# Turning the heads' outputs on VectorE and ScalarE instead of on TensorE, in a hybrid decoder block

## The chip, the core and the metric

The kernel runs on one core of one Trainium2 chip. The core has several engines that run at the same time, each through its own list of instructions in order: TensorE (matmuls, called PE in the profile, with its weight loads as PEld), VectorE (DVE), ScalarE (ACT), GpSimd (POOL) and SyncE (SP, here used to issue DMA transfers). They wait for each other through semaphores. SBUF is the on-chip memory with 128 partitions; PSUM holds what TensorE writes. The metric is the device time of one execution in microseconds (us), the median over several executions.

## The reference, cut to what matters

The block takes 512 tokens of width 1024, projects them, runs a gated short convolution beside an mLSTM branch with 4 heads, and merges the two. What the change touches is the output of a head: for each head an array of 512 tokens by 512 values, normalised, scaled by a gain per value (`g_head`) and multiplied by two gates, which is then the left factor of a projection.

```python
hb = mlstm_chunkwise(q, k, v, ig, fg)                  # (B, S, H, DV)
hb = rmsnorm(hb, g_head[l].reshape(N_HEADS, DV)).reshape(bsz, s, V_DIM)
yb = jax.nn.sigmoid(o) * hb * jax.nn.silu(zb)
yb = jnp.einsum('bsv,vd->bsd', yb, w_b_out[l])
```

For the last product TensorE contracts over partitions, so the values of a head have to lie on partitions and the tokens along the free dimension. The head itself is computed with tokens on partitions. Each head's 512x512 array therefore has to be transposed.

## The kernel before, in words

All matrix products are made to near fp32 accuracy from three products of rounded parts: each fp32 block is split into a high half (`whi`, ScalarE, L180) and a low half (`wlo`, VectorE, L181), and `mm3` (L233 to L235) multiplies high by high, high by low and low by high. The large products use Strassen's scheme with seven products of half-size blocks; its sums of weight blocks are made partly by accumulating DMAs of GpSimd (L156) and partly by VectorE (`wraw<-wraw`, L185). Weights come through four buffers `wraw`, filled by SyncE (L148).

The order on TensorE, ScalarE, VectorE and GpSimd is the order in which the program is written. It is written around ticks: after each step of matmuls (in the projection stages 12 matmuls of 512 columns, or 24 of 256 columns) `tick` is called. A tick emits, in this order, the first part of the pending sink of the step before (for instance a snapshot `s` or `v` of PSUM on ScalarE and a sum `c` on VectorE), one half of the next block's split, and one piece of each background task in the list `active`. A weight block has two halves and serves two steps, so its split runs one block ahead of the matmuls.

The turn of a head is such a background task. `finish` waits 2 ticks (even heads) or 3 (odd heads) after the head and then goes through `turn`, one piece per tick. Before the change the pieces are: eight TensorE transposes of 128x128 into two PSUM banks `pty` (L810); two scaled copies to SBUF on ScalarE (L805, the scale is `g_head` on partitions) and eight more transposes; two more scaled copies and the store of the turned head to DRAM by GpSimd (`yt_d<-yc`, L813). It is read back much later, in front of the projection.

Two buffers are shared in turn. `y`, the head's output with tokens on partitions (shown as `gty`), lies in the buffer tagged `qk`, and the next q/k block takes that buffer over. `yc`, the turned head, lies in the buffer tagged `vv`; after heads 0 and 2 the same buffer receives `qk_raw`, q and k of the next head read back from DRAM (the task `recut`, which waits 7 ticks, loads on SyncE and cuts into halves with `qk<-qk_raw` on ScalarE and VectorE).

What runs beside the turn: after an even head the Strassen product of the gate weights, whose weight sums are made by VectorE (L185) and whose results go through a sigmoid (`c<-c`, L781) to DRAM (`sg_d`, L782); after head 1 the q/k product of heads 2 and 3; after head 3 the first convolution product with its taps (L399, L401).

Of the kernel before, what the change touches and what calls it, by code (L numbers as in the profile page):

```python
# [9 lines left out]
F32 = mybir.dt.float32  # L10
F32R = mybir.dt.float32r
AF = mybir.ActivationFunctionType
ALU = mybir.AluOpType

P = 128
S = 512
NT = S // P
# [5 lines left out]
DV = 512  # L23
# [6 lines left out]
HC = 4  # L30
# [6 lines left out]
def hybrid_block(ctx, tc, x, p, g_mix, w_in, conv_w, conv_b, w_a_out, b_gates, g_head,  # L37
                 w_b_out, w_o, g_ple, w_ple_gate, w_ple, g_final, out):
    nc = tc.nc
    act, dve, pool, pe = nc.scalar, nc.vector, nc.gpsimd, nc.tensor  # L40
# [7 lines left out]
    ps_x = ctx.enter_context(tc.tile_pool(name="ps_x", bufs=4, space=bass.MemoryType.PSUM))  # L48
    dram = ctx.enter_context(tc.tile_pool(name="dram", bufs=1, space=bass.MemoryType.DRAM))

    def open_pool(name, bufs=1, **kw):
        c = tc.tile_pool(name=name, bufs=bufs, reuse_waits="tile", **kw)
        return c, c.__enter__()
# [16 lines left out]
    H2 = S // 2  # L70
# [182 lines left out]
    ident = const.tile([P, P], F32, name="ident")  # L253
# [270 lines left out]
    gh = prm[:, 40:56]  # L524
# [117 lines left out]
    for g in range(2):  # L642
        src = wg_raw[:, :, g * NH:(g + 1) * NH]
# [57 lines left out]
    B = nc.vector.STREAM_SQUARE_SIZE  # L701
# [96 lines left out]

    def turn(h, y):

        yc = hp.tile([P, 2, 2, HC, H2], F32, name="yc", tag="vv", align_bytes=256)[:, 0]
        pts = {}
        for i in range(3):
            for v in range(2 * i - 2, 2 * i) if i else ():
                act.activation(yc[:, :, v, :], pts[v].rearrange("p (h s) -> p h s", h=2), AF.Copy,  # L805
                               scale=gh[:, 4 * h + v:4 * h + v + 1])
            for v in range(2 * i, 2 * i + 2) if i < 2 else ():
                pts[v] = ps_x.tile([P, S], F32, name="pty", tag="x")
                for t in range(NT):
                    pe.transpose(pts[v][:, t * P:(t + 1) * P], y[:, t, v * P:(v + 1) * P], ident)  # L810
            if i < 2:
                yield
        nc.gpsimd.dma_start(yt_d[h], yc)  # L813

    def qk_tile():
# [181 lines left out]
    def finish(h, y, wait):  # L997
        for _ in range(wait):
            yield
        yield from turn(h, y)  # L1000

    hp_ctx, hp = open_pool("heads")
# [3 lines left out]
    for h in range(NH):  # L1006
        y = head(h, qks[h])
# [395 lines left out]
    q = [slice(CW, CW + CW // 2), slice(CW + CW // 2, D)]  # L1403
# [50 lines left out]
```

## Time and profile before

| | |
|---|---|
| time, median of 3 runs | 845.38 us (844.95 to 847.07) |
| profiled execution | 847.37 us, of which 845.6 us span from the first to the last instruction |
| granted TensorE clock | 0.998 |
| turns of heads 0 to 3, first transpose | 164.7, 257.7, 383.5, 476.5 us |
| stores of the turned heads, issue | 170.55, 266.06, 389.36, 483.29 us |

In rows of the profile a number at the front is the start in us from the first instruction, the next one the duration, then engine, source line, operation, output and inputs, and in square brackets how long the engine had been idle before and what ended that. "Chain of waits" is the chain of work that ended last, followed back from the end. Neighbouring instructions of VectorE and ScalarE can overlap a little, so from start to start they are closer than their durations. In a row of the view by stretches there stand the stretch and its length, then busy time and number of instructions for PE, PEld, DVE, ACT and POOL, the granted clock and the DMA share.

### The profile page before, as it was taken

The page shows a single profiled execution, that of the slowest core. Times are in us where ns is not written, and L with a number is a line of the kernel's source. Part 1 is how long each engine was busy: PE and PEld are TensorE (multiplying, and loading weights), DVE is VectorE, ACT ScalarE, POOL GpSimd, SP SyncE. Part 2 cuts the span into 40 slices and gives each one's busy share as a digit, 9 for nine tenths or more (in the row PEclk, how much of TensorE's full clock was granted, in tenths as well). Part 3 has the DMA queues.
Part 4 walks back from the last instruction along what each step waited for, and adds up shares of the span by engine and source line. Part 5 has one row for each costly group of instructions (what it writes and reads, how often), then busy time and mean ns, then how long its engine had stood idle before and what let it go on. Part 6 is the DMA issues. An engine that isn't in the chain of part 4 may idle for free.

```text
span 845.6 us, 12113 instructions
## 1 busy us (share of the span) xinstructions
PE 834.5 (99%) x4584; PEld 726.7 (86%) x4584; DVE 651.0 (77%) x878; ACT 495.5 (59%) x720; POOL 210.0 (25%) x203
## 2 busy tenths in 40 slices
PE   8999999999999999999999999999999999999996
PEld 7888888887889988888788999999998888888885
DVE  5788767975787677788668779897986677999565
ACT  6467665666865566665776654555453256667543
POOL 5203122203124321220222333433411122131031
PEclk9999999999999999999999999999999999999999
DMA  9748779779978997896898799899989488999402
GB/s 310 269 145 183 159 166 220 194 274 227 252 159 207 244 225 180 199 215 199 258 243 211 156 218 169 194 184 182 181 255 380 101 194 214 284 258 229 187 0 100
DMA packets 103939, 173.89 MB, mean 206 GB/s; under 512 B 5632, under 2 KB 46132, under 8 KB 102600
## 3 DMA queue, kind: packets, MB, share of 16 engines
q0 software_dynamic: 39488, 70.33, 44.6%
q1 hardware_dynamic: 59792, 94.64, 33.7%
q10 hardware_dynamic: 4600, 8.14, 3.1%
q8 instruction: 36, 0.59, 0.3%
q14 instruction: 23, 0.19, 0.1%
HBM read 156.30 MB, written 16.79 MB: 205 GB/s over the span
## 4 chain that ended last, share of the span: by engine, by line
PE 92%; DMA 3%; DVE 2%; issue 1%; ACT 1%; SPq 0%; POOL 0%; POOLq 0%; ACTq 0%; DVEq 0%
PE mm L234 28%; PE mm L235 28%; PE mm L233 28%; PE pv L233 1%; PE pv L235 1%; PE pv L234 1%; DMA wraw<-in_w_ple 1%; DMA wraw<-in_w_b_out 1%; PE pty L810 1%; DMA sg_d<-c 1%; PE sc L235 1%; PE sc L234 1%; PE sc L233 1%; DVE wlo L181 1%; PE ptk L1247 0%
## 5 line engine op out<-in xcount | busy, mean ns | idle before, releaser
L181 DVE TENSOR_TENSOR wlo<-wraw,whi 128x1024 fp32r<-128x1024 f32 x244 | 299.4, 1229 | 104.7 <-ACT whi L180 98.8
L180 ACT ACTIVATE whi<-wraw 128x1024 fp32r<-128x1024 f32 x246 | 257.1, 1054 | 103.8 <-PE mm L235 48.8
L156 POOL DMA_DIRECT2D wraw<-in_w_in x112 | 136.9, 1423 | 335.4 <-DVE wlo L181 207.7
L346 ACT ACTIVATE s<-mm 128x512 f32<-128x512 f32 x84 | 50.2, 597 | 100.2 <-PE mm L235 98.7
L233 PE MATMUL mm<-whi,hs 128*128 128x512 f32 x256 | 99.9, 390 | 0.0
L234 PE MATMUL mm<-wlo,hs 128*128 128x512 f32 x256 | 99.8, 390 | 0.0
L235 PE MATMUL mm<-whi,hs 128*128 128x512 f32 x256 | 99.7, 389 | 0.0
L233 PE MATMUL mm<-hn_hi,whi 128*128 128x256 f32 (+1 forms) x304 | 93.3, 307 | 0.0
L235 PE MATMUL mm<-hn_hi,wlo 128*128 128x256 f32 (+1 forms) x304 | 92.9, 306 | 0.0
L234 PE MATMUL mm<-hn_lo,whi 128*128 128x256 f32 (+1 forms) x304 | 92.8, 305 | 0.0
L233 PE MATMUL mm<-hs,whi 128*128 128x256 f32 x320 | 90.9, 284 | 0.0
L234 PE MATMUL mm<-hs,whi 128*128 128x256 f32 x320 | 90.5, 283 | 0.0
L235 PE MATMUL mm<-hs,wlo 128*128 128x256 f32 x320 | 90.5, 283 | 0.0
L234 PE MATMUL mm<-wlo,hn_hi 128*128 128x512 f32 x192 | 75.3, 392 | 0.4 <-DVE wlo L181 0.2
L233 PE MATMUL mm<-whi,hn_hi 128*128 128x512 f32 x192 | 74.9, 390 | 0.0
L235 PE MATMUL mm<-whi,hn_lo 128*128 128x512 f32 x192 | 74.8, 389 | 0.0
L234 PEld LDWEIGHTS mm<-hs,whi 128*128 128x128 f32 x320 | 61.4, 192 | 0.0
L233 PEld LDWEIGHTS mm<-hs,whi 128*128 128x128 f32 x320 | 61.4, 192 | 0.0
L235 PEld LDWEIGHTS mm<-hs,wlo 128*128 128x128 f32 x320 | 61.4, 192 | 0.0
L235 PEld LDWEIGHTS mm<-hn_hi,wlo 128*128 128x128 f32 x304 | 58.1, 191 | 2.5
L234 PEld LDWEIGHTS mm<-hn_lo,whi 128*128 128x128 f32 x304 | 58.1, 191 | 2.4
L233 PEld LDWEIGHTS mm<-hn_hi,whi 128*128 128x128 f32 x304 | 58.1, 191 | 2.4
(339 smaller groups left out, 1670.2 us busy)
## 6 DMA issues: line engine op xcount, KB each, us to landing
wraw<-in_w_in SPq DMA_DIRECT2D x32, 1024.0 KB, 6.1
wraw<-in_w_in POOLq DMA_DIRECT2D x52, 512.0 KB, 8.5
wraw<-in_w_in SPq DMA_DIRECT2D x48, 512.0 KB, 5.6
wraw<-in_w_in POOLq DMA_DIRECT2D x60, 256.0 KB, 5.7
wraw<-in_w_b_out SPq DMA_DIRECT2D x7, 1024.0 KB, 7.0
wraw<-in_w_b_out POOLq DMA_DIRECT2D x12, 512.0 KB, 7.0
wraw<-in_w_o SPq DMA_DIRECT2D x5, 1024.0 KB, 7.4
yt_d<-yc POOLq DMA_DIRECT2D x4, 1024.0 KB, 4.9
```

The source lines that it names most:

```text
L156: nc.gpsimd.dma_start(raws[to][:, ks, cs], src[:, ks, :], accum_op=ALU.add)
L180: act.activation(hi, t, AF.Copy)
L181: (e_lo or dve).tensor_tensor(lo, t, hi.bitcast(F32), ALU.subtract)
L233: pe.matmul(ps, lhsT=a[0], rhs=b[0], start=first, stop=False, **kw)
L234: pe.matmul(ps, lhsT=a[0], rhs=b[1], start=False, stop=False, **kw)
L235: pe.matmul(ps, lhsT=a[1], rhs=b[0], start=False, stop=last, **kw)
L346: act.activation(to[i], src, AF.Copy, scale=scale)
L810: pe.transpose(pts[v][:, t * P:(t + 1) * P], y[:, t, v * P:(v + 1) * P], ident)
```

## The change

`turn` no longer uses TensorE and PSUM. The 128x512 rows of a token tile are first transposed by VectorE in blocks of 32x32 (four instructions, two per tick, into the half `blocks` of the buffer). That leaves each 32x32 block turned in place, in the wrong quarter of the partitions. Sixteen copies of 32 partitions by 512 elements then carry each pair of quarters (from quarter b to quarter q, runs of 32 elements) to its place in the half `spread`: the eight with even number on ScalarE, the eight with odd number on VectorE, eight of the sixteen per tick. In the next tick ScalarE makes four copies with the scale `g_head` back into `blocks`, and GpSimd stores that. A turn takes five ticks instead of three.

```diff
     def turn(h, y):
 
-        yc = hp.tile([P, 2, 2, HC, H2], F32, name="yc", tag="vv", align_bytes=256)[:, 0]
-        pts = {}
-        for i in range(3):
-            for v in range(2 * i - 2, 2 * i) if i else ():
-                act.activation(yc[:, :, v, :], pts[v].rearrange("p (h s) -> p h s", h=2), AF.Copy,
-                               scale=gh[:, 4 * h + v:4 * h + v + 1])
-            for v in range(2 * i, 2 * i + 2) if i < 2 else ():
-                pts[v] = ps_x.tile([P, S], F32, name="pty", tag="x")
-                for t in range(NT):
-                    pe.transpose(pts[v][:, t * P:(t + 1) * P], y[:, t, v * P:(v + 1) * P], ident)
-            if i < 2:
+        both = hp.tile([P, 2, NT, DV], F32, name="yc", tag="vv", align_bytes=256)
+        spread, blocks = (both[:, i] for i in range(2))
+        for t in range(NT):
+            dve.transpose(blocks[:, t, :], y[:, t, :])
+            if t % 2:
                 yield
+        for i in range((P // B) ** 2):
+            b, q = divmod(i, P // B)
+            src = blocks[b * B:(b + 1) * B].rearrange("p t (v q a) -> p t v q a", q=P // B, a=B)[:, :, :, q]
+            dst = spread[q * B:(q + 1) * B].rearrange("p v (t b a) -> p t v b a", b=P // B, a=B)[:, :, :, b]
+            if i % 2:
+                dve.tensor_copy(dst, src)
+            else:
+                act.activation(dst, src, AF.Copy)
+            if i % 8 == 7:
+                yield
+        yc = blocks.rearrange("p t v -> p (t v)").rearrange("p (h v s) -> p h v s", h=2, v=HC)
+        for v in range(HC):
+            act.activation(yc[:, :, v, :], spread[:, v, :].rearrange("p (h s) -> p h s", h=2), AF.Copy,
+                           scale=gh[:, HC * h + v:HC * h + v + 1])
         nc.gpsimd.dma_start(yt_d[h], yc)
```

The order on the engines changes at these places. First VectorE at the turn of head 0, beside the gate product, before the change (`wlo` rows are splits, `wraw<-wraw` rows the sums of gate weights, numbers behind names count the tiles):

```order
L181 TENSOR_TENSOR wlo_1517<-wraw_1189,whi_1516 128x1024
L185 TENSOR_TENSOR wraw_1189<-wraw_1189,wraw_1357 128x1024
L350 TENSOR_TENSOR c<-s,mm 128x512
L181 TENSOR_TENSOR wlo_1548<-wraw_1189,whi_1547 128x1024
L185 TENSOR_TENSOR wraw_1189<-wraw_1189,wraw_1357 128x1024
L350 TENSOR_TENSOR c<-s,mm 128x512
L181 TENSOR_TENSOR wlo_1580<-wraw_1357,whi_1579 128x1024
L185 TENSOR_TENSOR wraw_1403<-wraw_1403,wraw_1357 128x1024
L181 TENSOR_TENSOR wlo_1605<-wraw_1357,whi_1604 128x1024
L185 TENSOR_TENSOR wraw_1403<-wraw_1403,wraw_1357 128x1024
L181 TENSOR_TENSOR wlo_1628<-wraw_1189,whi_1627 128x1024
```

And the same place after the change (`STREAM_TRANSPOSE` is the block transpose, `COPY` the move between quarters):

```order
L185 TENSOR_TENSOR wraw_1189<-wraw_1189,wraw_1357 128x1024
L804 STREAM_TRANSPOSE yc<-gty 128x512 x2
L350 TENSOR_TENSOR c<-s,mm 128x512
L181 TENSOR_TENSOR wlo_1540<-wraw_1189,whi_1539 128x1024
L185 TENSOR_TENSOR wraw_1189<-wraw_1189,wraw_1357 128x1024
L804 STREAM_TRANSPOSE yc<-gty 128x512 x2
L350 TENSOR_TENSOR c<-s,mm 128x512
L181 TENSOR_TENSOR wlo_1562<-wraw_1357,whi_1561 128x1024
L185 TENSOR_TENSOR wraw_1403<-wraw_1403,wraw_1357 128x1024
L812 COPY yc<-yc 32x4x4x32 x4
L181 TENSOR_TENSOR wlo_1592<-wraw_1357,whi_1591 128x1024
L185 TENSOR_TENSOR wraw_1403<-wraw_1403,wraw_1357 128x1024
```

The transposes stand in front of the sums `c`, the moves between a sum of gate weights and the next split; behind the second row of `wraw_1403` four more moves follow.

ScalarE at the same place after the change; before it, each pair of splits had two scaled copies `yc<-pty` behind it and no moves:

```order
L180 ACTIVATE whi_1561<-wraw_1357 128x1024
L814 ACTIVATE yc<-yc 32x4x4x32 x4
L781 ACTIVATE c<-c 128x512
L782 DMA sg_d_96<-c 128x512
L346 ACTIVATE v<-mm 128x512
L180 ACTIVATE whi_1591<-wraw_1357 128x1024
L814 ACTIVATE yc<-yc 32x4x4x32 x4
L781 ACTIVATE c<-c 128x512
L782 DMA sg_d_96<-c 128x512
L346 ACTIVATE v<-mm 128x512
L180 ACTIVATE whi_1622<-wraw_1189 128x1024
L819 ACTIVATE yc<-yc,prm 128x2x256 x4
```

The moves stand behind one split and ahead of the gate's sigmoid, the snapshot `v` and the next split; the four scaled copies stand between the splits of the two halves of one block (`whi_1622` and, behind the copies, `whi_1644`).

SyncE's loads around the reload of q and k after head 0, as a difference:

```order
-L825 DMA qk_raw<-qk_d_94 128x512
-L148 DMA wraw_1609<-in_w_in 128x4x512
-L825 DMA qk_raw<-qk_d_94 128x512 x3
+L148 DMA wraw_1596<-in_w_in 128x4x512
 L148 DMA wraw_1649<-in_w_in 128x4x512
+L833 DMA qk_raw<-qk_d_94 128x512 x4
 L148 DMA wraw_1692<-in_w_in 128x4x512
```

The reload now stands behind two weight loads instead of one ahead of them and one between its pieces; the same holds after head 2.

## Prediction

> **What bounds the kernel now.** I read the busy shares and the chain of waits first, then who waits on the TensorE queue, then the stretches in which the heads are turned.
>
> ```profile
> PE 834.5 (99%) x4584; PEld 726.7 (86%) x4584; DVE 651.0 (77%) x878; ACT 495.5 (59%) x720; POOL 210.0 (25%) x203
> ...
> PE 92%; DMA 3%; DVE 2%; issue 1%; ACT 1%; SPq 0%; POOL 0%; POOLq 0%; ACTq 0%; DVEq 0%
> ```
>
> TensorE is busy 99% of the span and makes 92% of the chain. Work taken off it is time gained, as long as its operands still arrive.
>
> ```profile
> PE mm L234 <- DVE wlo L181: 0.2, 1, 0.2
> ...
> PEld mm L234 <- DVE wlo L181: 2.7, 6, 0.7
> ```
>
> The longest waits of the matmuls and weight loads on `wlo`, the low half of a split weight block: six weight-load waits, 2.7 us. So everything else is hidden today, but does it have room?
>
> ```profile
> 162.00:190.00 28.00, 28.00 (x133) 23.37 (x132) 22.61 (x23) 17.50 (x24) 0.55 (x1) 1.00 0.69 228
> 254.00:276.00 22.00, 22.00 (x188) 22.00 (x186) 15.58 (x18) 11.71 (x16) 10.73 (x10) 1.00 0.88 206
> ```
>
> These stretches (columns PE, PEld, DVE, ACT, POOL) hold the turn of head 0 and of head 1. VectorE works 22.61 of 28 us in the first: 5.4 us idle. Head 2 repeats head 0's pattern, head 3 resembles head 1 with the convolution's taps in place of the q/k cuts.
>
> **What is removed.**
>
> ```profile
> 164.90 0.87 PE pty L810 x8
> ...
> 257.88 0.87 PE pty L810 x8
> 261.62 0.87 PE pty L810 x8
> ...
> 480.24 0.87 PE pty L810 x8
> ```
>
> Each group of eight transposes takes 0.87 us of the chain: 8 groups, 6.96 us, 1.74 per head. If nothing else moved, the profiled execution's 847.4 (span 845.6) would become 840.4 and the median 845.4 would become 838.4.
>
> **What is added.** Per head VectorE gets 4 block transposes of 128x512 and 8 moves of 32x512; ScalarE gets 8 moves and keeps 4 scaled copies, now from SBUF.
>
> ```profile
> L891 DVE STREAM_TRANSPOSE pp<-pp x4: 705/706/706, 103.7 to 450.1; 128x512 f32<-128x512 f32 x4
> ...
> L895 DVE COPY pp<-pp x12: 162/163/167, 107.8 to 454.5; 32x16 f32<-32x16 f32 x12
> ...
> L1390 DVE TENSOR_SCALAR y<-xg,fs x2: 488/489/490, 830.2 to 831.9; 128x512 f32<-128x512 f32 x2
> ...
> L1388 ACT ACTIVATE y<-xg,fs x2: 710/716/722, 837.8 to 841.1; 128x512 f32<-128x512 f32 x2
> ...
> L559 DVE COPY ple<-mmp x1: 692/692/692, 9.9 to 9.9; 128x512 f32<-128x512 f32 x1
> ```
>
> A block transpose is 0.71 us (L891 is the same shape), spaced 0.62 since neighbours overlap by some 0.08. A move of 512 elements has no row. From below: L895, a move between quarters of 16 elements, costs 0.16; from above: the 512-element copy from PSUM, L559, 0.69. Nearest is L1390: one source, both ends in SBUF, 512 elements, 0.49. [...] VectorE's addition is 4 x 0.62 + 8 x 0.49 = 6.4 us per head, more than the 5.4 idle. ScalarE's moves go by the 0.62 us of a same-sized SBUF copy, spaced 0.52 (both in the rows for ScalarE below); its scaled copies by L1388, 0.72, spaced 0.6.
>
> [...]
>
> **Where it lands, head 0.** Each tick of the schedule gives VectorE one `wlo` half, and TensorE uses a block's first half at a step's start and the second half six matmuls later.
>
> ```profile
> 171.96 0.39 PE L233 MATMUL mm<-whi,hs 128*128 128x512 f32 x1
> ...
> 174.68 0.39 PE L233 MATMUL mm<-whi,hs 128*128 128x512 f32 x1
> ```
>
> A step is 12 matmuls, 2.72 us. Call the steps A, B and so on; C starts at 171.96, D at 174.68, so B at 169.2, F at 180.1, H at 185.6, J at 191.0, and B, D, F, H, J begin on new blocks. Without transposes and without stalls B would start at 167.5, D at 172.9, F at 178.4, H at 183.8. The low halves are needed one and seven matmuls into the step: 0.23 and 1.59 us.
>
> ```profile
> 163.79 1.23 DVE L181 TENSOR_TENSOR wlo<-wraw,whi 128x1024 fp32r<-128x1024 f32 x1 [0.82 <-ACT whi L180]
> 165.05 1.22 DVE L185 TENSOR_TENSOR wraw<-wraw,wraw 128x1024 f32<-128x1024 f32 x1
> 166.19 0.68 DVE L350 TENSOR_TENSOR c<-s,mm 128x512 f32<-128x512 f32 x1
> 166.79 1.22 DVE L181 TENSOR_TENSOR wlo<-wraw,whi 128x1024 fp32r<-128x1024 f32 x1
> ...
> 174.88 1.22 DVE L185 TENSOR_TENSOR wraw<-wraw,wraw 128x1024 f32<-128x1024 f32 x1
> 176.46 1.23 DVE L181 TENSOR_TENSOR wlo<-wraw,whi 128x1024 fp32r<-128x1024 f32 x1 [0.36 <-ACT whi L180]
> 177.72 1.23 DVE L185 TENSOR_TENSOR wraw<-wraw,wraw 128x1024 f32<-128x1024 f32 x1
> ```
>
> Split and add take 1.26 + 1.14 us from start to start, a product with `c` 0.60. In these ticks VectorE already spends 2.4 to 3.0 of 2.72 us, because the sums of the gate weights (L185) are made there, and the changed order puts the new work between those rows: two transposes, two transposes, four moves, four moves. I replay it from 163.79 with these durations.
>
> Split, add, two transposes, `c`: B's second half starts at 168.0 and is ready at 169.3, needed 169.1. Add, two transposes, `c`: D's first half starts at 172.3, ready 173.5. Add until 174.7, four moves until 176.6: D's second half is ready at 177.9, needed 174.5.
>
> ```profile
> 172.16 0.60 ACT L346 ACTIVATE v<-mm 128x512 f32<-128x512 f32 x1 [1.38 <-PE mm L235]
> 172.65 1.05 ACT L180 ACTIVATE whi<-wraw 128x1024 fp32r<-128x1024 f32 x1
> ...
> 187.20 0.62 ACT L240 ACTIVATE qk<-qk_raw 128x512 fp32r<-128x512 f32 x1
> 187.72 0.62 ACT L781 ACTIVATE c<-c 128x512 f32<-128x512 f32 x1
> ...
> 188.75 0.60 ACT L346 ACTIVATE s<-mm 128x512 f32<-128x512 f32 x1 [0.40 <-PE mm L235]
> 189.24 1.05 ACT L180 ACTIVATE whi<-wraw 128x1024 fp32r<-128x1024 f32 x1
> ```
>
> ScalarE says the same: its first four moves cannot start before the last transpose ends, 171.7, then 2.1 us of moves, 1.04 for the gate's sigmoid and its DMA issue (187.72 to 188.75), 0.5 for the snapshot, and only then the split of D's second half, until 176.3. In the profile that split began at 172.65. So D stops 3 us.
>
> Then add and four moves until 181.1, F's first half ready 182.3. The four scaled copies wait for VectorE's moves (181.1) and run until 183.4; F's second high half is behind them on ScalarE, split until 184.4, its low half ready 185.7. In the profile its place was 180.1 + 1.59 = 181.7. **Head 0 loses 4.0 us**, net of the transposes; after that VectorE's load falls to 1.9 us a tick and H is met. With 0.42 a move it is 3.7 (ScalarE's order holds it), with 0.69 5.5. Head 2: the same.
>
> **Heads 1 and 3.**
>
> ```profile
> 258.31 0.68 DVE L350 TENSOR_TENSOR c<-s,mm 128x512 f32<-128x512 f32 x1
> 258.91 1.22 DVE L181 TENSOR_TENSOR wlo<-wraw,whi 128x1024 fp32r<-128x1024 f32 x1
> ...
> 263.19 0.69 DVE L241 TENSOR_TENSOR qk<-c,qk 128x512 fp32r<-128x512 f32 x1 [1.93 <-ACT qk L240]
> 264.63 1.23 DVE L181 TENSOR_TENSOR wlo<-wraw,whi 128x1024 fp32r<-128x1024 f32 x1 [0.74 <-ACT whi L180]
> ```
>
> ```profile
> 262.53 0.63 ACT L240 ACTIVATE qk<-c 128x512 fp32r<-128x512 f32 x1 [2.90 <-PE pty L810]
> ```
>
> The transposes now stand around the `c` of 258.31. `qk<-c` on ScalarE takes over the buffer that the turn reads, so it waited for TensorE's last transpose and now waits for VectorE's: 258.31 + 1.24, `c`, split, add, 1.24 more makes 263.7. Cut, snapshot and split follow on ScalarE: a high half at 265.9, its low half at 267.1. Add and four moves to 270.3, `qk` 270.9, the next low half 272.1, four moves 274.1, and the one after that is ready at 275.4. Its place in the profile: the step is 2.87 us here (258.75 to 261.62 in the chain above), three steps after 262.5 is 271.1, and the second half is due 0.84 us later, 271.9. **Head 1 loses 3.5 us** (3.0 and 5.2 at the ends).
>
> ```profile
> 484.14 0.68 DVE L420 TENSOR_TENSOR cu<-c 128x512 f32<-128x512 f32 x1
> ...
> 486.74 0.35 DVE L399 TENSOR_SCALAR cv<-cu,prm 128x256 f32<-128x256 f32 x1
> 487.12 1.00 DVE L401 SCALAR_TENSOR_TENSOR cv<-cu,prm,cv 128x256 f32<-128x256 f32 x2
> ```
>
> Head 3 has no such wait, but the moves stand with `cu` and the taps (0.35 + 1.00) ahead of the splits: second transposes to 482.3, split 483.5, add and moves 486.7, `cu` 487.3, split 488.6, moves 490.5, taps 491.8, split ready 493.1. Its place was 481.1 + 3 x 2.87 + 0.84 = 490.5. **Head 3 loses 2.6 us** (2.0 and 4.2).
>
> **The reload behind it.** In even heads the q/k reload uses the turned tile's buffer, so it waits for the store.
>
> ```profile
> yt_d<-yc POOLq DMA_DIRECT2D x4, 1024.0 KB, 4.9
> ```
>
> ```profile
> DMA to landing us min/median/max: 3.6/6.3/7.5
> ```
>
> The first row is the store's size and median time to landing, the second the reload's. The store now follows the scaled copies, 183.5, and lands 4.9 us later at 188.4, the reload's first piece 3.6 to 7.5 after that: 192.0 to 195.9. ScalarE cuts it 1.64 us after G ends (187.20 in the profile, now 191.2); behind that cut stands the split of J's second half (189.24). That one is ready at 189.24 + 1.05 + 1.23 = 191.5 and due at 192.6, so the wait, minus this 1.1, costs TensorE 0 to 3.6 us. I take 1.2, since the first of four pieces should land early. Two weight loads that go ahead of the reload on SyncE lose nothing; the one now behind it belongs to a block two operands later, 2 x 5.4 us of matmuls, which covers it.
>
> **Sum.** 4.0 + 3.5 + 4.0 + 2.6 = 14.1; reloads 2 x 1.2 = 2.4; about 1.0 of today's 2.7 us of `wlo` waits is swallowed by the delay: 15.5 us, already net of the 6.96. On the profiled execution 862.9, on the median **861**. Lower end of every term: 3.7 x 2 + 3.0 + 2.0 - 1.0 = 11.4, 857. Upper end: 5.5 x 2 + 5.2 + 4.2 + 7.2 = 27.6, 873.
>
> **Rivals.**
> 1. *The cover holds (838.4).* VectorE and ScalarE run far enough ahead that `wlo` is never late: 845.4 - 7.0. For it: TensorE waits for almost nothing now, the others are busy 77% and 59%, and the turn needs no PSUM bank any more. It decides if the halves have over 4 us of slack; the replay shows 1 to 4, and 6.4 us of work does not fit 5.4 of idle time. Chance 0.10.
> 2. *Even (845.9).* The odd heads are covered (-1.74 each), the even ones lose half of mine (+2.0 each): +0.5, no change that can be told. For it: head 1's stretch has 6.4 of 22 us idle on VectorE. Against: ScalarE's wait for the reused buffer, which idle time on VectorE does not shorten. Chance 0.07.
> 3. [...] Chance 0.15.
> 4. *The reload at its worst (866).* 3.6 instead of 1.2 in both even heads: 15.5 + 4.8 = 20.3. For it: pieces of one issue share the queues. Chance 0.08.
>
> [...]
>
> Forecast 861: chance 0.60, own range 856 to 867. A measurement of this kernel tells about 0.3% (2.5 us) from no change. Faster 0.10 (rival 1), same 0.07 (rival 2), slower 0.83. The range 850 to 872 leaves out rivals 1 and 2.
>
> **What would show it.** Right: no `pty` rows; in each head two or more gaps of 1 to 4 us on TensorE released by `wlo` L181, in even heads at D's and F's second halves; VectorE without idle time from 164 to 185; moves of 0.42 to 0.5 us; TensorE's idle time up from 11 us by about 22; `yc` on ScalarE waiting for VectorE. [...] A move that costs ScalarE well over 0.62 us would break the sum upwards, since ScalarE's chain sets the even heads.

## The result, and the profile after

The changed kernel takes **871.00 us** (median of 6 runs, 868.58 to 873.13) against 845.69 us before (median of 6, 844.95 to 847.07): 2.98% slower, ratio 1.0298 with a 95% interval of 1.0279 to 1.0317. The forecast was slower, 861, range 850 to 872. The direction and the mechanism came as forecast. Of the 25.3 us lost, the sum had 15.5.

The page of the changed kernel, its busy times and its chain of waits:

```profile
PE 838.5 (96%) x4520; PEld 723.3 (83%) x4520; DVE 674.8 (78%) x926; ACT 516.7 (59%) x752; POOL 209.8 (24%) x203
...
PE 74%; issue 7%; DVE 7%; DMA 6%; ACT 4%; POOL 0%; SPq 0%; ACTq 0%; POOLq 0%; DVEq 0%
```

The profiled execution took 871.88 us, its span is 870.1 against 845.6. TensorE has 64 instructions less and yet is busy 4 us longer (why is told with the clock, in the section on the prediction). It now stands idle 31.6 us of the span (870.1 - 838.5), 11.1 before. Its share of the chain falls from 92% to 74%; VectorE, ScalarE and transfers, which made 6% of it, now make 17%. The groups of new instructions (line, operation, count, busy time, mean ns):

```profile
L814 ACT ACTIVATE yc<-yc 32x512 f32<-32x512 f32 x32 | 20.1, 629 | 10.3 <-DVE yc L804 10.0
L812 DVE COPY yc<-yc 32x512 f32<-32x512 f32 x32 | 13.9, 434 | 0.5
L804 DVE STREAM_TRANSPOSE yc<-gty 128x512 f32<-128x512 f32 x16 | 10.4, 685 | 0.0
L819 ACT ACTIVATE yc<-yc,prm 128x512 f32<-128x512 f32 x16 | 10.2, 712 | 0.1
```

They were bought to save 8 x 0.87 = 6.96 us of TensorE; they cost 24.3 us of VectorE and 30.3 us of ScalarE. Of the latter 10.1 us were there before, as the scaled copies from PSUM. Who makes the matmuls wait (us in total, times, longest):

```profile
PE mm L234 <- DVE wlo L181: 5.7, 9, 1.4
PE mm L233 <- ACT v L346: 5.6, 5, 1.6
PE mm L235 <- DVE wlo L181: 3.8, 4, 2.1
PE mm L233 <- DVE c L350: 3.4, 4, 1.1
PE mm L233 <- ACT whi L180: 1.6, 2, 0.9
```

The low halves (9.5 us) are there as forecast; before there were 0.2 us of such waits of matmuls. But nearly as much is waited for the snapshots `v` and the sums `c`, which clear PSUM banks: they stand in the same late queues, and the forecast did not look at them. In head 0 TensorE stops six times, 5.0 us in all, and only 1.1 of these are waits for `wlo`: by the time that a low half is due, `c` or `v` has already held the step up. The last three of the six:

```profile
178.40 0.50 PE L234 MATMUL mm<-wlo,hs 128*128 128x512 f32 x1 [0.32 <-DVE wlo L181]
...
181.36 0.50 PE L233 MATMUL mm<-whi,hs 128*128 128x512 f32 x1 [1.54 <-ACT v L346]
...
186.97 0.50 PE L234 MATMUL mm<-wlo,hs 128*128 128x512 f32 x1 [0.76 <-DVE wlo L181]
```

Head 0 on VectorE:

```profile
170.59 1.30 DVE L804 STREAM_TRANSPOSE yc<-gty 128x512 f32<-128x512 f32 x2
171.81 0.65 DVE L350 TENSOR_TENSOR c<-s,mm 128x512 f32<-128x512 f32 x1
...
174.74 1.71 DVE L812 COPY yc<-yc 32x512 f32<-32x512 f32 x4
177.12 1.23 DVE L181 TENSOR_TENSOR wlo<-wraw,whi 128x1024 fp32r<-128x1024 f32 x1 [0.66 <-ACT whi L180]
...
179.51 1.72 DVE L812 COPY yc<-yc 32x512 f32<-32x512 f32 x4
182.29 1.22 DVE L181 TENSOR_TENSOR wlo<-wraw,whi 128x1024 fp32r<-128x1024 f32 x1 [1.06 <-ACT whi L180]
...
185.69 1.23 DVE L181 TENSOR_TENSOR wlo<-wraw,whi 128x1024 fp32r<-128x1024 f32 x1 [0.91 <-ACT whi L180]
```

and on ScalarE:

```profile
171.92 2.56 ACT L814 ACTIVATE yc<-yc 32x512 f32<-32x512 f32 x4 [4.26 <-DVE yc L804]
174.51 0.63 ACT L781 ACTIVATE c<-c 128x512 f32<-128x512 f32 x1
...
175.54 0.60 ACT L346 ACTIVATE v<-mm 128x512 f32<-128x512 f32 x1 [0.40 <-PE mm L235]
176.04 1.05 ACT L180 ACTIVATE whi<-wraw 128x1024 fp32r<-128x1024 f32 x1
177.11 2.55 ACT L814 ACTIVATE yc<-yc 32x512 f32<-32x512 f32 x4
...
181.21 1.05 ACT L180 ACTIVATE whi<-wraw 128x1024 fp32r<-128x1024 f32 x1
182.16 2.55 ACT L819 ACTIVATE yc<-yc,prm 128x512 f32<-128x512 f32 x4
184.61 1.99 ACT L180 ACTIVATE whi<-wraw 128x1024 fp32r<-128x1024 f32 x2
...
194.89 0.63 ACT L240 ACTIVATE qk<-qk_raw 128x512 fp32r<-128x512 f32 x1 [2.19 <-DMA qk_raw<-qk_d]
```

VectorE waits for ScalarE before each of the three splits shown: ScalarE's chain of moves, sigmoid, snapshot and high half sets this head, as the forecast had it. D's second low half is ready at 178.35 (177.12 + 1.23; forecast 177.9), F's at 186.92 (185.69 + 1.23; forecast 185.7). Its four moves take 2.56 us, 0.64 each, where the forecast spaced them by 0.52. The last row is the reload: the cut waits 2.2 us for it.

**Where the time goes.** The same split can be found in both traces, and its delay read off. For one of them, before and after:

```profile
254.12 1.22 DVE L181 TENSOR_TENSOR wlo<-wraw,whi 128x1024 fp32r<-128x1024 f32 x1
```

```profile
261.08 1.22 DVE L181 TENSOR_TENSOR wlo<-wraw,whi 128x1024 fp32r<-128x1024 f32 x1
```

The delay is 7.0 us. The table has the delay at seven such splits for the change and for every kernel of the experiments (us against the trace of before; the column heads say what lies just ahead of the split and when it starts in the trace of before; differences along a row are what a piece costs).

| kernel | turn 0, 187.34 | reload, 254.12 | turn 1, 371.63 | turn 2, 405.94 | reload, 440.84 | start of head 3, 469.48 | turn 3, 505.75 |
|---|---|---|---|---|---|---|---|
| the change | 5.4 | 7.0 | 11.9 | 17.1 | 19.5 | 20.3 | 25.2 |
| no moves | 0.6 | 2.8 | 3.8 | 4.2 | 6.4 | 7.1 | 5.9 |
| odd heads only | -0.1 | -0.4 | 3.0 | 3.0 | 2.5 | 2.3 | 6.2 |
| even heads only | 5.0 | 7.9 | 7.9 | 13.3 | 14.6 | 14.4 | 14.4 |
| odd heads, spread | -0.1 | -0.8 | 4.2 | 4.2 | 3.5 | 3.6 | 4.6 |
| fillers | 4.7 | 7.0 | 10.4 | 15.6 | 17.0 | 17.1 | 19.5 |
| reload apart | 6.7 | 9.8 | 13.2 | 18.6 | 18.5 | 19.5 | 23.4 |
| spread and late | 0.7 | 6.8 | 10.6 | 11.1 | 17.5 | 18.2 | 19.2 |
| moves on VectorE | 8.1 | 8.7 | 17.2 | 25.8 | 26.9 | 27.6 | 34.7 |
| moves on ScalarE | 10.7 | 12.0 | 22.1 | 33.7 | 35.5 | 36.4 | 42.6 |
| transposes put back | 4.9 | 6.7 | 11.6 | 16.8 | 18.5 | 18.4 | 22.2 |
| no reload | 4.8 | 4.1 | 7.5 | 12.6 | 12.9 | 13.6 | 17.5 |
| even heads on GpSimd | 1.0 | 3.4 | 3.5 | 4.8 | 7.7 | 9.3 | 9.3 |

For the change: 0.2 at the start, then head 0's turn 5.2, its reload 1.6, head 1's turn 4.9, head 2's 5.2, its reload 2.4, 0.8 at the start of head 3, head 3's turn 4.9; 0.7 is given back in the last stages. Together 24.5, the difference of the spans.

### The profile page after: what moved, and what is told of

Its sections match the earlier page's. It is cut to its first block, busy times and chain, and to the rows that moved or that the text cites. A ratio compares the mean times of both kernels' runs of the same rounds, so it can differ in the third digit from the quotient of the medians.

```text
span 870.1 us, 12061 instructions
## 1 busy us (share of the span) xinstructions
PE 838.5 (96%) x4520; PEld 723.3 (83%) x4520; DVE 674.8 (78%) x926; ACT 516.7 (59%) x752; POOL 209.8 (24%) x203
## 4 chain that ended last, share of the span: by engine, by line
PE 74%; issue 7%; DVE 7%; DMA 6%; ACT 4%; POOL 0%; SPq 0%; ACTq 0%; POOLq 0%; DVEq 0%
PE mm L235 23%; PE mm L234 23%; PE mm L233 22%; DMA wraw<-in_w_in 3%; DVE wlo L181 2%; ACT whi L180 1%; DMA gty<-z_d 1%; PE pv L234 1%; PE pv L235 1%; PE pv L233 1%; ACT yc L814 1%; DMA wraw<-in_w_ple 1%; DVE yc L804 1%; DMA qk_raw<-qk_d 1%; DVE gty L972 1%
## 5 line engine op out<-in xcount | busy, mean ns | idle before, releaser
L181 DVE TENSOR_TENSOR wlo<-wraw,whi 128x1024 fp32r<-128x1024 f32 x244 | 299.3, 1228 | 106.0 <-ACT whi L180 100.2
L235 PE MATMUL mm<-hs,wlo 128*128 128x256 f32 x320 | 92.8, 290 | 3.8 <-DVE wlo L181 3.8
L233 PE MATMUL mm<-hs,whi 128*128 128x256 f32 x320 | 93.0, 291 | 3.0 <-ACT whi L180 1.6
L234 PE MATMUL mm<-hs,whi 128*128 128x256 f32 x320 | 92.3, 289 | 0.0
L235 PEld LDWEIGHTS mm<-hs,wlo 128*128 128x128 f32 x320 | 63.4, 198 | 4.6 <-DVE wlo L181 4.6
L233 PEld LDWEIGHTS mm<-hs,whi 128*128 128x128 f32 x320 | 63.3, 198 | 4.1 <-ACT whi L180 2.2
L233 PEld LDWEIGHTS mm<-whi,hs 128*128 128x128 f32 x256 | 48.1, 188 | 21.4 <-ACT v L346 6.1
L234 PEld LDWEIGHTS mm<-hs,whi 128*128 128x128 f32 x320 | 63.3, 198 | 0.0
```

The costliest lines, as they stand in the source:

```text
L181: (e_lo or dve).tensor_tensor(lo, t, hi.bitcast(F32), ALU.subtract)
L233: pe.matmul(ps, lhsT=a[0], rhs=b[0], start=first, stop=False, **kw)
L234: pe.matmul(ps, lhsT=a[0], rhs=b[1], start=False, stop=False, **kw)
L235: pe.matmul(ps, lhsT=a[1], rhs=b[0], start=False, stop=last, **kw)
```

## Experiments

### What the moves cost, and what the rest

```diff
-            if i % 2:
-                dve.tensor_copy(dst, src)
-            else:
-                act.activation(dst, src, AF.Copy)
+            pass
...
-            act.activation(yc[:, :, v, :], spread[:, v, :].rearrange("p (h s) -> p h s", h=2), AF.Copy,
+            act.activation(yc[:, :, v, :], blocks[:, v, :].rearrange("p (h s) -> p h s", h=2), AF.Copy,
```

> As the change, but the 16 moves between partition quarters of each head are left out: the scaled copies read the block-transposed tile straight, so features and tokens of the heads' outputs are not in their places. Block transposes, scaled copies, store and reload stay. Theory (VectorE and ScalarE are late in the ticks that hold eight moves): those ticks lose 3.4 us on VectorE and 5.1 us on ScalarE per head, the waits on wlo L181 go back to under 0.5 us each, TensorE's idle time is 12 to 16 us and the time 846 to 850 us. Rival (the transposes, or the chain store and reload, cost most of it): 860 us or more, with waits on wlo or on the reload still of 1 us and more.

Measured: 852.42 us (ratio to before 1.0074, 1.0056 to 1.0092). The moves cost 18.6 of the 25.3 us. The rest is more than expected, and the table says where it is: the turns of heads 0 and 2 cost 0.5 and 0.4, but the reload behind each 2.2. Even without moves the store comes late, since the scaled copies still stand in the fifth tick: head 0's is issued at 179.81, against 170.55 before and 185.00 in the change. The rival's 860 is out; the expectation's upper end is passed by 2.4 us. TensorE's idle time is 19.8 us where 12 to 16 were expected, and the longest wait of a matmul for `wlo` still 1.3 us where it was to fall under 0.5.

### Odd heads alone, even heads alone

```diff
+    def turn(h, y):
+        return (turn_new if h % 2 else turn_old)(h, y)
```

> The odd heads (1 and 3) are turned in the new way, the even ones by TensorE transposes as before. Theory, from the lags between the two traces: head 1 costs 5.3 us, head 3 about 4, so 854 to 857 us; the clock of the TensorE still falls after both turns, since it follows from these heads' own gaps. Rival A (the clock falls because of what the even heads did before, or because of the delay as a whole): 850 us and a clock of 1.00 behind the turns. Rival B (terms as predicted, 3.5 + 2.6): 852 us.

> The even heads (0 and 2) are turned in the new way, the odd ones by TensorE transposes as before. Theory, from the lags: 5.2 + 5.1 for the turns and 1.3 to 2 each for the reload, so 858 to 861 us, clock 1.00 throughout. With the odd-only kernel's excess it adds up to the whole change's 25.3 us within 2 us. Rival (terms as predicted, 4.0 x 2 + 1.2 x 2 = 10.4): 856 us. Rival (the heads are not independent): the two excesses add up to under 22 or over 28 us.

Measured: odd heads only 854.03 us (1.0090, 1.0073 to 1.0107), even heads only 862.34 us (1.0191, 1.0174 to 1.0208). The excesses over the 846.24 of that comparison are 7.8 and 16.1, together 23.9 of 25.3: the heads add up. The odd heads cost 3.4 and 3.9 where the lags said 5.3 and 4, and the clock falls in both turns here too (to 0.50 from 266.9 and from 495.6), with the old even heads: it comes from these heads' own gaps (rival A is out). The even heads cost 1.3 us more than the upper end; here the clock fell once, in head 2 (to 0.50 from 407.6), where it had not in the whole change.

### Spreading the odd heads' moves

```diff
-            if i % 8 == 7:
+            if i % 4 == 3:
                 yield
...
+        return (turn_new if h % 2 else turn_old)(h, y)
```

> The odd heads in the new way with four moves to a tick (two on each engine) in place of eight, over four ticks in place of two; the even heads by TensorE transposes as before. Theory (what costs is the bunching in two ticks: split and four moves are 1.26 + 1.7 of 2.87 us of VectorE beside the sums; with two moves a tick has 0.4 us to spare): 847 to 851 us, and no drop of the clock behind the turns. Rival (the amount of work counts, not how it is spread): within 1 us of the odd-only kernel.

Measured: 851.24 us (1.0053, 1.0038 to 1.0068), 2.8 less than with eight moves to a tick. Head 3 does what was expected: 1.0 us in place of 3.9. Head 1 does not: 5.0 in place of 3.4. A row of VectorE in this kernel:

```profile
289.09 0.69 DVE L350 TENSOR_TENSOR c<-s,v 128x512 f32<-128x512 f32 x1 [6.00 <-DMA qk_d<-c]
```

The 1 MB store of the turned head is issued at 278.97, right ahead of two stores of `qk_d` on the same queue, and VectorE waits 6 us for the buffer `c` that these read. With eight moves to a tick the store went out at 276.51, 2.6 us ahead of the first of them, and there is no such wait. TensorE idles for 1.85 us of one window and the clock falls (0.995 granted over the execution, 0.998 before), against the expectation. Of all kernels with the new turn in some heads this is the fastest, and still 0.5% slower than before.

### All heads spread, and later

```diff
-            if i % 8 == 7:
+            if i % 4 == 3:
...
-        active.append(finish(h, y, 2 + h % 2))
+        active.append(finish(h, y, 3 if h % 2 else 6))
```

The reload is also changed, as in "The reload apart" below.

> The same work, placed elsewhere: four moves to a tick in all heads, the even heads' turn four ticks later (behind most of the sums of the gate weights, L185), the reload in buffers of its own. Theory (the cost is the VectorE and ScalarE load of the ticks in which the work was put): the even heads lose 0 to 1.5 us each, head 1 some 4 (its store meets the stores of qk_d, as in the kernel with the odd heads' moves spread), head 3 some 1: 848 to 854 us. Rival (the amount of work on VectorE and ScalarE costs this wherever it stands): 865 us or more.

Measured: 867.25 us (1.0254, 1.0239 to 1.0270). The theory falls for the even heads. Up to 187 it holds, 0.7 us; by 254 it is 6.8. Behind the sums of the gate weights VectorE has room, but ScalarE has none: there its ticks hold the cut of the reload, two sigmoids and their DMA issues.

```profile
196.67 2.55 ACT L819 ACTIVATE yc<-yc,prm 128x512 f32<-128x512 f32 x4
199.12 0.62 ACT L240 ACTIVATE qk<-qk_raw 128x512 fp32r<-128x512 f32 x1
199.64 0.62 ACT L781 ACTIVATE c<-c 128x512 f32<-128x512 f32 x1
...
201.66 1.06 ACT L180 ACTIVATE whi<-wraw 128x1024 fp32r<-128x1024 f32 x1 [0.40 <-ACT sg L781]
```

TensorE stops 2.5 us for this `whi`, in head 2 too, and the clock falls behind both (0.994 granted over the execution; in head 2 matmuls of 512 columns start 0.43 us apart from 433.44, 0.23 ahead of the stop). So in the even heads neither place has room on both engines: where VectorE is free ScalarE is full. That is what the rival said, though with one engine after the other as its reason.

### One engine for all moves

```diff
-            if i % 2:
-                dve.tensor_copy(dst, src)
-            else:
-                act.activation(dst, src, AF.Copy)
+            dve.tensor_copy(dst, src)
```

and the same with `act.activation(dst, src, AF.Copy)` alone.

> The change, with all 16 moves of a head on VectorE. A batch of eight then takes 8 x 0.42 = 3.4 us on VectorE in place of 1.7, and ScalarE is free of its 2.56. Theory (ScalarE's moves hold the split's high half, but VectorE's queue is as full): the even heads' D and F each get 1.7 us later on VectorE and no longer wait for ScalarE's moves, so 0 to 2 us more per head, 871 to 879 us. Rival (ScalarE alone sets it, as the prediction's sentence on the order of ScalarE has it): 862 us or less.

> The change, with all 16 moves of a head on ScalarE, spaced 0.64 us there: a batch of eight takes 5.1 us in place of 2.56, and VectorE is free of its 1.7. Theory (in the even heads ScalarE's chain sets D and F: sigmoid, snapshot and the split's high half stand behind the moves; all on VectorE cost 11 us more, 2.7 of it in head 0): each batch puts the high half behind it 2.55 us later, so 5 us more per head and 20 in all, less what the odd heads have spare, 885 to 893 us. Rival (VectorE's queue sets it, so that taking its moves away pays): 870 us or less.

Measured: all on VectorE 882.32 us (1.0433, 1.0416 to 1.0451), all on ScalarE 890.23 us (1.0527, 1.0508 to 1.0545). Neither engine has room for the other's half. On ScalarE the time is within the expectation. On VectorE it is 3 us more than the upper end: the four turns lose 2.7, 3.6, 3.4 and 2.2 us more than in the change, where 0 to 2 were expected, and the clock falls behind each turn (0.983 granted over the execution; in head 0 it is 0.50 from 178.7 and from 188.9). The matmuls' longest waits, on VectorE and then on ScalarE:

```profile
PE mm L235 <- DVE wlo L181: 12.7, 6, 5.4
```

```profile
PE mm L233 <- ACT v L346: 18.8, 7, 4.1
```

With the moves on ScalarE head 0 loses 5.3 us more than in the change (10.7 - 5.4), what two batches of 2.55 us make: in the even heads ScalarE's queue passes its moves on to TensorE in full.

### Was TensorE's work worth anything?

```diff
             if t % 2:
+                for _ in range(2):
+                    pt = ps_x.tile([P, S], F32, name="pty", tag="x")
+                    for k in range(NT):
+                        pe.transpose(pt[:, k * P:(k + 1) * P], y[:, k, :P], ident)
                 yield
```

> The change, with TensorE's 16 transposes per head put back as idle work: in the two ticks of VectorE's block transposes, out of the same tile, into PSUM banks that nobody reads (8 groups of 0.87 us, 6.96 us of TensorE). Theory (TensorE waits in these ticks for VectorE and ScalarE anyway, so what was taken from it buys next to nothing): 870 to 873.5 us, with TensorE's idle time down by about what is put back. Rival (the transposes' removal did buy its 6.96 us, and the losses are that much larger): 876 to 879 us.

Measured: 869.80 us (1.0285, 1.0262 to 1.0307), no different from the change within some 2.5 us. TensorE's idle time falls from 31.6 to 25.7 us (868.6 - 842.9), about what was put back. In the ticks of the block transposes TensorE has to wait for `c` anyway. In the change and with the transposes put back:

```profile
172.52 0.50 PE L233 MATMUL mm<-whi,hs 128*128 128x512 f32 x1 [1.12 <-DVE c L350]
```

```profile
168.12 1.03 PE L809 MATMUL pty<-ident,gty 128*128 128x128 f32 x8
172.06 0.50 PE L233 MATMUL mm<-whi,hs 128*128 128x512 f32 x1 [0.17 <-DVE c L350]
```

The gap shrinks by what is put into it. So the 6.96 us that were to be gained went into new waits: TensorE does less and waits that much longer.

### The reload

```diff
-        raw = hp.tile([P, 2, 4, S], F32, name="qk_raw", tag="vv", align_bytes=256)[:, 0]
-        for m in range(4):
-            nc.sync.dma_start(raw[:, m, :], qk_d[h][:, m, :])
...
-            cut(qk[0][:, m, :], qk[1][:, m, :], raw[:, m, :])
+            cut(qk[0][:, m, :], qk[1][:, m, :], hn_hi[:, m, :].bitcast(F32))
```

> The change, with the q/k reload of the even heads left out: the four loads are gone and the cuts read a tile that is always there, so the odd heads' scores are wrong. Theory (in each even head the cut waits for the reload, which waits for the store): 1.6 us less in head 0, 2.4 in head 2, 866 to 868 us, give or take 1.7 for a clock drop that comes or goes; the waits of ScalarE for qk_raw are gone. Rival (that wait is hidden): 870 to 872 us.

Measured: 866.54 us (1.0241, 1.0224 to 1.0258), 4.5 less than the change. In the table the two reload steps fall from 1.6 and 2.4 to -0.7 and 0.3. The first cut no longer waits:

```profile
192.00 0.62 ACT L240 ACTIVATE qk<-hn_hi 128x512 fp32r<-128x512 f32 x1
```

At 192.00 in place of 194.89. The reload behind the store is worth some 2.2 us in each even head.

**The reload apart.**

```diff
+        raw = []
+        def load(m):
+            raw.append(hp.tile([P, S], F32, name="qk_raw", tag="raw", bufs=2, align_bytes=256))
+            nc.sync.dma_start(raw[m], qk_d[h][:, m, :])
+        load(0)
+        load(1)
...
+            if m < 2:
+                load(m + 2)
```

> The change, with the q/k reload of the even heads in two small buffers of its own, so that it no longer waits for the store of the turned tile; two pieces are loaded early, the other two after the first cuts. Theory (the reload behind the store costs 1.6 to 2.4 us in each even head): 3.2 to 4.8 us less, 866 to 868 us, give or take 1.7 us for a clock drop that comes or goes. Rival (the reload's wait is hidden, the cost is the turn's own): 870 to 872 us.

Measured: 870.72 us (1.0292, 1.0276 to 1.0307), no gain. It does not contradict the run above but does not serve: behind head 2 the step is gone (-0.1), behind head 0 it is 3.1, of which a fall of the clock at 211.8 makes up to 1.7 (half of the 3.41 us that the fall at 413.2 lasts), and only two of four pieces are early: the fourth cut still waits for its piece, 2.6 us in head 0 and 2.1 in head 2. A buffer for all four was not tried.

### GpSimd for the moves

```diff
-            if i % 2:
-                dve.tensor_copy(dst, src)
-            else:
-                act.activation(dst, src, AF.Copy)
-            if i % 8 == 7:
-                yield
+            pool.tensor_copy(dst, src)
+        for _ in range(8):
+            yield
...
+        return (turn_new if h % 2 == 0 else turn_old)(h, y)
```

> The even heads in the new way with all 16 moves on GpSimd, which is idle in these stretches, and the scaled copies eight ticks later, one to a tick; the reload in buffers of its own; the odd heads by TensorE transposes as before. Compared with the kernel with only the even heads changed (862.3 us, 16.1 above before). Theory (the even heads lose by the moves' load on VectorE and ScalarE): without it each even head loses 0.6 us by the transposes and up to 2 by the scaled copies among the cuts, 847 to 851 us. Rival (GpSimd's copies slow VectorE down, or come too late for the store): 855 us or more, with L181 rows well over 1.23 us.

Measured: 856.37 us (1.0127, 1.0110 to 1.0144): by the ratios 5.4 us better than the same heads with the moves on VectorE and ScalarE, but 5 above the expectation. The turn itself costs little (1.3 us in head 0 and in head 2); the rest is lost behind it. What the rival names is there. GpSimd, in head 0 and then over both heads (ns: shortest, median, longest), and VectorE before and during its copies:

```profile
171.56 22.09 POOL L811 COPY yc<-yc 32x512 f32<-32x512 f32 x16 [12.49 <-DVE yc L804]
```

```profile
L811 POOL COPY yc<-yc x32: 599/1508/1692, 171.6 to 414.5; 32x512 f32<-32x512 f32 x32
```

```profile
168.89 1.23 DVE L185 TENSOR_TENSOR wraw<-wraw,wraw 128x1024 f32<-128x1024 f32 x1
...
177.81 1.62 DVE L181 TENSOR_TENSOR wlo<-wraw,whi 128x1024 fp32r<-128x1024 f32 x1
...
185.56 0.68 DVE L350 TENSOR_TENSOR c<-s,mm 128x512 f32<-128x512 f32 x1
186.16 1.22 DVE L181 TENSOR_TENSOR wlo<-wraw,whi 128x1024 fp32r<-128x1024 f32 x1
```

While GpSimd copies, until 193.65, most splits and sums take 1.62 us in place of 1.23; `c<-s,mm`, which has one input in PSUM, takes its usual 0.68. It goes the other way too: most of GpSimd's copies take 1.51 us, but the one beside the `c<-s,mm` of 187.41 takes 0.61, and the one that begins together with the split of 186.16, which keeps its 1.22, takes 1.69. How much of the 5 us that makes, beside the scaled copies among the cuts and a fall of the clock at 429.8 (0.995 granted over the execution), was not separated.

### Filling the gaps of the odd heads

```diff
+        if h % 2:
+            pt = ps_x.tile([P, S], F32, name="fill", tag="x")
+            for k in range(24 if h == 3 else 12):
+                pe.transpose(pt[:, k % NT * P:(k % NT + 1) * P], ident, ident)
         yc = blocks.rearrange("p t v -> p (t v)").rearrange("p (h v s) -> p h v s", h=2, v=HC)
```

> The change, plus idle work for TensorE behind the moves of the odd heads: 12 transposes of a constant (head 1) and 24 (head 3) into PSUM banks that nobody reads, queued just ahead of the block that waited. Theory (a 3.41 us window in which TensorE idles some 1.6 us or more halves its clock in the next; that costs the change 1.7 us behind head 1 and 2.8 behind head 3): the fillers run inside the gaps (1.5 and 2.95 us there), the clock stays at 1.00 behind these turns, and the time falls by 2 to 4.5 us, to 866.5 to 869. Rival (the clock drop costs nothing, since the splits behind it are late anyway, or it has another cause): 870.5 to 872 us. Rival (the fillers lie on the path): up to 3.9 us longer, 872 to 875.

What it is about: behind head 1 and head 3 the matmuls of the change run at half speed. Stretches of 3.41 us of the change (PE busy first, PEclk the third number from the end):

```profile
279.95:283.36 3.41, 1.91 (x14) 1.50 (x13) 1.96 (x3) 3.41 (x6) 2.42 (x4) 0.98 0.79 95
283.36:286.77 3.41, 3.41 (x18) 3.41 (x18) 1.91 (x2) 2.48 (x3) 2.12 (x3) 0.52 1.10 138
409.54:412.95 3.41, 1.85 (x9) 1.20 (x8) 2.27 (x6) 2.98 (x5) 0.00 (x0) 1.00 0.56 135
412.95:416.36 3.41, 3.41 (x15) 2.37 (x13) 2.46 (x3) 3.41 (x6) 0.54 (x1) 1.00 0.66 249
508.54:511.95 3.41, 1.69 (x12) 1.28 (x11) 3.23 (x9) 3.31 (x6) 2.44 (x2) 0.99 0.62 128
511.95:515.36 3.41, 2.18 (x10) 2.18 (x11) 3.34 (x6) 2.19 (x4) 1.93 (x3) 0.50 0.88 120
515.36:518.78 3.42, 3.42 (x18) 3.42 (x18) 1.09 (x3) 1.55 (x2) 1.10 (x2) 0.51 1.08 143
```

In the first and the fifth TensorE waits 1.5 and 1.7 us, and the granted clock is 0.5 in the next window, or the next two. (The third waits as long, and the clock behind it is 1.00; what sets it apart is in the last section.) Measured with the fillers: **868.57 us** (1.0268, 1.0253 to 1.0283), 2.4 less than the change; the profiled span is 865.5 against 870.1, 4.6 less. The clock stays at 1.00 in both places:

```profile
279.36 1.47 PE L820 MATMUL fill<-ident 128*128 128x128 f32 x12
```

```profile
285.00:290.00 5.00, 5.00 (x44) 5.00 (x43) 4.12 (x5) 2.54 (x4) 1.98 (x3) 1.00 1.11 246
...
515.00:520.00 5.00, 5.00 (x44) 5.00 (x43) 3.80 (x6) 3.60 (x5) 0.00 (x0) 1.00 1.06 362
```

The matmul behind the last wait of head 1's turn starts at 282.20 in the change and at 282.24 with the fillers, so they lie inside the gap and what they save comes behind it. Turn 1 costs 3.4 in place of 4.9, turn 3 2.4 in place of 4.9: 4.0 us of the profiled execution are the clock's. 36 transposes that nobody needs make the kernel faster, by 2.4 us between the medians (the two intervals just overlap), less than the 4.6 between the spans. The granted clock of the four runs with fillers goes from 0.993 to 0.998, so which windows fall differs from run to run, and the share of the clock in the median was not fixed more closely than by these two numbers.

## Why the prediction was right, and where its sum was short

Direction and place were right, and so was the mechanism, operands that come late. Of the profiled 24.5 us 9.0 were missing: the sum left the clock out and priced ScalarE's moves and the reload too low. 871.0 lies above the forecast's own range of 856 to 867 and only just inside the wider one of 850 to 872. By the forecast's own steps:

| step | forecast | measured in the profile |
|---|---|---|
| head 0 | 4.0 | 5.2 |
| head 1 | 3.5 | 3.4, and 1.5 by the clock |
| head 2 | 4.0 | 5.2 |
| head 3 | 2.6 | 2.4, and 2.5 by the clock |
| reloads | 2 x 1.2 | 1.6 + 2.4 |
| swallowed by the delay | -1.0 | -0.7, given back only behind 700 us |
| not foreseen: the start of the trace and of head 3 | 0 | 0.2 + 0.8 |

- **Nothing for nothing.** That TensorE's 6.96 us could only be had if the operands came in time was the core of it, and putting the transposes back shows it most plainly: they cost nothing that can be measured. Rivals 1 (838.4) and 2 (845.9) fall; the odd heads were not covered either.
- **Price of VectorE's moves.** The sum has 0.49; the rows of the change say 0.416 to 0.423 for all but two of 32 (these 0.66). No row of the trace of before shows the 0.42 of the sum's lower end; the moves came out at it. The upper end's 0.69 (L559) is out.
- **The even heads: the mis-sized term is ScalarE's moves.** "Spaced 0.52" was read from neighbours of 128 partitions; the moves run 0.64 apart, so a batch of four takes 2.56 and not 2.1. Two batches stand ahead of F's second half: 1.0 of the 1.2 us missing per head, and the scaled copies do start at 182.16 in place of 181.1. That ScalarE's queue passes its moves on in full is shown by the run with all moves on it (5.3 us more in head 0); VectorE's lies close behind, since all moves on VectorE cost 2.7 us more there. The forecast's own warning, a move on ScalarE well over 0.62 a piece, was right in its direction and looked at the duration instead of the spacing.
- **The odd heads.** 3.5 and 2.6 were within 0.2 us, once the clock is held. Head 1's `qk<-c` waited for VectorE's transposes as replayed (5.6 us in the profile). The replay's last low halves, at 275.4 and 493.1, plus the delays of 7.0 and 20.3 that were there before these turns, make 282.4 and 513.4; TensorE went on at 282.20 and 513.18. So these two terms were not hit by luck.
- **The clock is the step that is missing altogether.** The sum took a stop as costing its length. 4.0 us of the profile come on top of it, none of them next to a wait row: they show only in the granted clock and in matmuls 0.21 apart where they were 0.12. They also explain a part of why TensorE is busy longer with less to do: with the fillers, where the clock stays, it is busy 838.1 us, of which 4.2 are the fillers, so some 4.6 of the 838.5 are the clock's, while 11 are to be explained (838.5 against 834.5 less 6.96). The rest was not traced; behind a wait the profile shows a matmul at 0.50 us in place of 0.39.
- **The reload.** 1.2 was taken from a range of 0 to 3.6. It measures 2.0 per head in the trace and 2.2 by leaving it out; rival 4 (3.6) is not borne out either. The store went out at 185.0 (forecast 183.5), and "the first of four pieces should land early" did not hold: the first cut starts at 194.89 where the forecast's order had it at 191.2.
- **The swallowed waits.** The 1.0 was a part of 2.7 us that weight loads waited for `wlo`, while the matmuls themselves waited only 0.2 us for it. There was next to nothing to swallow at that place; what is given back lies behind 700 us.
- **Signs.** No `pty` rows, idle time of TensorE up by 20.5 us (forecast 22), `yc` on ScalarE waiting for VectorE: right. Gaps released by `wlo` at D's and F's second halves: right in place (178.40 and 186.97), but 0.3 and 0.8 us long there where 1 to 4 were forecast, and only 9.5 us of the waits are named after `wlo`, the others after `v`, `c` and `whi`. VectorE without idle time from 164 to 185: wrong by 1.7 us before two splits, in which it waited for ScalarE.
- **Open:** the 0.8 us at the start of head 3, where VectorE waited 2.5 us for a load (`gty<-z_d`); it is 0.1 with the fillers. Why those loads were late was not tried.

## What to carry to other kernels

Work taken off the busiest engine is worth only what the engines that feed it can afford, tick by tick: look for a place where every receiving queue has room at once, and here there was none in the even heads. Price moved instructions by their spacing in the same pattern (same partitions, same neighbours), not by the duration or spacing of a similar one (here 0.64 us on ScalarE where 0.52 was taken). And once a saturated TensorE starts to wait, count the clock: here 1.5 and 1.7 us of waits in one stretch of 3.41 us were followed by a clock of 0.5, which cost 1.5 and 2.5 us more.

## What the runs showed of the hardware that was not expected

- **The clock fell behind windows in which TensorE was up to 40% full, not idle.** In eleven kernels the clock fell between 150 and 550 us, in eight of them more than once; there the falls of one run lie a multiple of 3.413 us apart (for the change 283.22 and 511.91, 67 windows), and each lasts whole windows at 0.5 (for the change 3.41 and 6.83 us). Counting the columns of the matmuls that start in each window at full clock (some 1,240 windows): the 28 with at most 3,072 were all followed by a window at 0.5, and none of those with 3,328 or more; a full window holds about 7,680. The kernel with the fillers, whose clock did not fall there, has one window with 3,072 (from 176.95) that goes unpunished, so 3,072 is seen with either outcome. The fillers count: without their columns two of its windows, from 279.35 and 504.63, would have 3,072 and 2,048, and the clock behind both is 1.00. So in these runs it is neither the length of one gap (0.76 us was the longest in the window behind head 1, and the unpunished one at 409.54 has one of 1.56) nor the busy time: the window at 409.54 above is busy 1.85 us, less than that at 279.95, but 7 matmuls of 512 columns start in it, in the other 11 of 256, and it is not punished. None of these 28 windows was idle, and the longest wait of a matmul in the change is 2.1 us.
- **ScalarE's moves between partition quarters did not overlap.** Four 32x512 moves take 2.56 us at 0.629 each; the four scaled copies over all partitions behind them take 2.55 at 0.712 each, so these do overlap. VectorE's moves do not either: 1.71 for four of 0.42. Whether the change of quarters or the 32 partitions are the cause was not told apart.
- **GpSimd's copies and VectorE held each other up, but only where both inputs of VectorE's instruction are in SBUF.** L181 and L185 mostly take 1.62 in place of 1.23 us, `c<-s,v` 1.09 and `qk<-qk_raw,qk` 1.10 in place of 0.68, `c<-s,mm` 0.68 as ever; GpSimd's copies take 0.60 at the least and mostly 1.51. Where both have work without a break they take turns: between 173 and 178 us VectorE starts an instruction every 1.55 us, and GpSimd a copy every 1.55 us.
